# A third block product done in seven smaller ones, over two feature tiles

## The chip, the cores and the metric

The kernel runs on one core of a Trainium2 chip. The metric is the device time of one execution in microseconds, as the median of several runs. Its engines are TensorE (PE in the profile, with PEld for its weight loads), VectorE (DVE), ScalarE (ACT), GpSimd (POOL) and SyncE (SP), which here issues the DMAs. Every engine works through its own instructions in order and waits on semaphores for the others.

## What is computed

One inference step of a hybrid decoder layer on 1048 tokens (16 learned ones, 1024 of a prompt, 8 samples) of width 1024. The layer has a half-step feed-forward block, a mixing block (HGRN2 and Mamba-2 heads) and a second half-step feed-forward block. The change lies in the two feed-forward blocks (FFN), which are

```python
def rmsnorm(x, w):
    xf = x.astype(jnp.float32)
    y = xf * lax.rsqrt(jnp.mean(xf * xf, axis=-1, keepdims=True) + EPS)
    return (y * w.astype(jnp.float32)).astype(x.dtype)

def swiglu(x, wg, wu, wd):
    return (jax.nn.silu(x @ wg) * (x @ wu)) @ wd
...
    h = h + 0.5 * swiglu(rmsnorm(h, n1), w1g, w1u, w1d)
...
    h = h + 0.5 * swiglu(rmsnorm(h, n2), w2g, w2u, w2d)
```

with `wg` and `wu` (1024, 2816) and `wd` (2816, 1024), all in float32. So there are 22 feature tiles of 128 columns in `wg` and `wu`.

## The kernel before

**Numbers.** Each float32 operand is split into a high part (a cast to the format that TensorE takes, on ScalarE) and a low part (the difference, on VectorE). A product is three matmuls, high by high, high by low and low by high: `mm3`, lines 163 to 165.

**Gate and up in block form.** For one feature tile, gate and up together are a 2 by 2 block product: the left side is gate and up by the two halves of the 1024 input features (four raw weight blocks of 128 by 512), the right side the input by the same halves and by two parts of the tokens. `Left`, `Unit` and `pair` do this with Strassen's seven block products instead of eight (in Winograd's arrangement): `ORDER = (1, 6, 2, 5, 7, 3, 4)`, line 334. The right operands and their sums are made once (`Blocks`) and stay, 28 slots of the ring "u" with 30 slots; one more holds the scaling of the norm (`Spread`). Left operands 1, 7, 4 and 2 are the raw blocks, 5, 6, 7 and 3 are sums of them (`Left.sum_`, L482). Each block product is done for two token halves c = 0 and 1, a step each: 4 row tiles × 3 matmuls = 12 matmuls of 262 columns (258 in the second FFN). A feature tile has 14 steps.

**The order.** `Steps` is a list of steps. `S.before(i, fn)` puts work ahead of step i, `post` comes right behind a step's matmuls, and jobs of one step come in the order in which they were registered. VectorE, ScalarE, TensorE and SyncE keep this order (`manual_schedule` in `ffn`). For a tile that begins at step s0, `Left.plan` puts the loads at s0−11 and s0−10, the sums at s0−7 to s0−5, the cast of the k-th product (`hi`, L486) at s0+2k−4 and its low part (`lo`, L490) one step later.

**Evacuation.** Product sums lie in PSUM, in two pairs of banks (`psum2`) while gate and up run; products 2, 3 and 4 add to the banks of 1, 5 and 7 after these have been read. `post` in `pair`: product 1 is copied (ScalarE, L574), 6, 5, 7, 3 and 4 are added to what is there (VectorE, L576, L583, L585, L587, L593), gate and up are scaled by `spread` (L569), silu runs on ScalarE (L581, L602), and the products go to the hidden slots (L608). `Hidden` forms four sums of the hidden blocks of two tiles (L734) and stores seven blocks (L737), from which the down product's operands are loaded later (`Hidden.load`, with low parts of 1048 columns at L762).

**Rings.** Raw weights "r" 8 slots, temporaries "t" 9, split weights "ws" 6, "s" 8 (hidden blocks and their sums). Four more PSUM banks (`psm`) aren't used by steady gate and up.

**Loops.** `ffn` runs over 11 pairs of feature tiles. In the first FFN, pair 0 is done without Strassen's form (`Plain`) and pairs 1 to 10 by `pair`; in the second all 11 go through `pair`, the first tile in another order (`first`). Then `down` follows; its first operand loads and low parts are put into the last steps of gate and up (14 to 2 steps ahead).

Of the kernel before, what the change touches and what calls it, by code (L numbers as in the profile page):

```python
# [9 lines left out]
F32 = mybir.dt.float32  # L10
F32R = mybir.dt.float32r
# [6 lines left out]
P = 128  # L18
# [421 lines left out]
class Steps:  # L440
# [9 lines left out]
    def add(self, mm, post=None):  # L450
        self.steps.append((mm, post))

    def run(self):
        for i, (mm, post) in enumerate(self.steps):
            for fn in self.at.pop(i, ()):
                fn()
            mm()
            if post:
                post()
        for i in sorted(self.at):  # L460
            for fn in self.at[i]:
                fn()


class Left:

    def __init__(self, K, srcs, n):
        self.K, self.n = K, n  # L470
        self.srcs = dict(zip((1, 7, 4, 2), srcs))
        self.raw, self.w = {}, {}

# [4 lines left out]
    def sum_(self, p):  # L478
        x, y, op = {5: (7, 4, ALU.add), 6: (5, 1, ALU.subtract), 7: (1, 7, ALU.subtract), 3: (2, 6, ALU.subtract)}[p]
        if p not in self.raw:  # L480
            self.raw[p] = self.K.raw(self.n * P)
        self.K.nc.vector.tensor_tensor(self.raw[p], self.raw[x], self.raw[y], op)  # L482

    def hi(self, p):
# [8 lines left out]
        self.hi(p)  # L493
        self.lo(p)

    def plan(self, S, s0, late, sums):
        for ps, ds, fn in (
            ((1, 7, 4, 2), (-11, -11, -10, -10), self.load),
            ((5, 6, 7, 3), [d + sums for d in (-7, -7, -6, -5)], self.sum_),
            (ORDER, [2 * i - 4 + late for i in range(7)], self.hi),  # L500
            (ORDER, [2 * i - 3 + late for i in range(7)], self.lo),
        ):
            for p, d in zip(ps, ds):
                S.before(s0 + d, lambda p=p, fn=fn: fn(p))
# [9 lines left out]
class Unit:  # L514


    def __init__(self, K, w, ops, n, post):
        self.K, self.w, self.ops, self.n, self.post = K, w, ops, n, post
        self.ps = {}

    def bank(self, p, cs, mis):
# [10 lines left out]
    def step(self, S, p, c, cs, mis=False):  # L532
        def mm():
            new = p in (1, 6, 5, 7)
            b = self.bank(p, cs, mis)
            product(self.K, b[:, cs.index(c)], self.w[p], self.ops[c][p], self.n, new, True, not new)

        S.add(mm, (lambda: self.post(p, slice(cs[0], cs[-1] + 1), self.bank(p, cs, mis))) if c == cs[-1] else None)

    def both(self, S):  # L540
        for p in ORDER:
# [158 lines left out]
            S.before(at + i, lambda fn=fn, n=n: fn(n))  # L700


FP = DFF // P // 2

DORDER = (1, 5, 6, 7, 3, 4, 2)
# [3 lines left out]
class Hidden:  # L709
# [6 lines left out]
    def jobs(self, S, i, hid, e0, e1):  # L716

        K = self.K
        t, b = {}, {}

        def block(n):

            return hid[n // 2][0][:, n % 2 * 2 * self.K.Q : n % 2 * 2 * self.K.Q + 2 * self.K.Q]

        def val(p):
            return b[p] if p in b else block({1: 0, 12: 1, 2: 2, 3: 3}[p])

        def sub(p, x, y):
# [5 lines left out]
            K.nc.vector.tensor_sub(b[p], val(x), val(y))  # L734

        def store(p):
            K.nc.sync.dma_start(self.d[p][:, :, i, :], halves(val(p)))  # L737

        ks = (1, 3, 5) if i < FP - 1 else (1, 2, 3)
        for at, args in zip((e0 + 1, *(e1 + k for k in ks)), ((5, 12, 1), (6, 3, 5), (7, 3, 12), (4, 2, 6))):  # L740
            S.before(at, lambda args=args: sub(*args))
            S.before(at + 2, lambda p=args[0]: store(p))
        for at, p in ((e0 + 2, 1), (e1 + 1, 3), (e1 + 2, 2)):
            S.before(at, lambda p=p: store(p))

    def load(self, S, p, at):

# [147 lines left out]
def ffn(K, wg, wu, wd, ops, spread, src, first, after, late_r, plain=False):  # L895
# [1385 lines left out]
```

## Time and profile before

| | us |
|---|---|
| median of 3 runs (1946.39 to 1948.55) | 1947.09 |
| span of the profiled execution | 1943.5 |
| TensorE busy in the span | 1921.7 |
| TensorE weight loads busy | 1887.7 |
| VectorE busy | 1434.7 |
| ScalarE busy | 823.6 |
| GpSimd busy | 90.3 |

The profile is of one execution; the page gives its span, from the first to the last instruction, and no time of its own. Busy TensorE is modelled from the starts of matmuls, so 99% says that it always has work, not that it is at its peak. The granted clock is 0.997 over the span. In a row of the order of time stand the start, the length, the engine, the line, the operation, what it writes and reads, and in brackets how long the engine had been idle and who released it. "x2" merges two neighbours, with the length of both.

### The profile page before, as it was taken

To read this page: it belongs to the slowest core of one execution; us is meant where nothing else is said; L and a number is where in the kernel's file an instruction comes from. 1 tells how busy PE (TensorE), PEld (TensorE's weight loads), DVE (VectorE), ACT (ScalarE), POOL (GpSimd) and SP (SyncE) were. 2 spreads that over 40 slices of the span, in tenths; PEclk is the share of its full clock that TensorE was granted. 3 is DMA by queue.
4 is the path that set the end of the run, shared out by engine and by line. 5 is a ranking of instruction groups with operands and counts; after the bars stand their busy time and mean duration, and the time that the engine had idled before them with its cause. 6 is when DMAs were issued, how large, how long until landed. Compare 5 with 4: busy or idle time off the path is not lost.

```text
span 1943.5 us, 41139 instructions
## 1 busy us (share of the span) xinstructions
PE 1921.7 (99%) x16800; PEld 1887.7 (97%) x16800; DVE 1434.7 (74%) x2516; ACT 823.6 (42%) x1558; POOL 90.3 (5%) x144
## 2 busy tenths in 40 slices
PE   9999999999999999999999999999999999999998
PEld 8999999999999999999899999999999999999998
DVE  7877777778688877576575556987777777768974
ACT  7522222224543644466564545742222222354343
POOL 3000000000000510000000002200000000000000
PEclk9999999999999999999999999999999999999999
DMA  8142332325977541221453254223332433487852
GB/s 246 47 129 83 101 114 83 114 85 157 289 230 257 172 146 53 64 88 48 117 160 93 79 176 137 91 80 99 94 104 82 124 90 100 153 257 231 280 182 86
DMA packets 324207, 258.45 MB, mean 133 GB/s; under 512 B 18923, under 2 KB 298731, under 8 KB 324011
## 3 DMA queue, kind: packets, MB, share of 16 engines
q1 hardware_dynamic: 323779, 255.79, 43.4%
q8 instruction: 132, 2.16, 0.4%
q14 instruction: 56, 0.46, 0.1%
q0 software_dynamic: 224, 0.04, 0.0%
q10 hardware_dynamic: 16, 0.00, 0.0%
HBM read 190.79 MB, written 65.05 MB: 132 GB/s over the span
## 4 chain that ended last, share of the span: by engine, by line
PE 93%; DVE 4%; issue 1%; ACT 1%; DMA 1%; SPq 0%; POOL 0%; DVEq 0%; ACTq 0%; POOLq 0%
PE acc L163 29%; PE acc L164 28%; PE acc L165 28%; PE mis L1677 1%; PE mis L1390 0%; DVE u L376 0%; PE mis L1739 0%; PE mis L1384 0%; DMA s<-in_x_prompt_dram 0%; DVE ws L490 0%; DVE t L321 0%; PE mis L1768 0%; PE mis L1377 0%; PE mis L1668 0%; PE mis L223 0%
## 5 line engine op out<-in xcount | busy, mean ns | idle before, releaser
L163 PE MATMUL acc<-u,ws 128*128 128x258 f32 (+3 forms) x4514 | 1316.4, 292 | 5.6 <-DVE t L583 2.3
L165 PE MATMUL acc<-u,ws 128*128 128x258 f32 (+3 forms) x4514 | 1304.0, 289 | 1.3 <-DVE ws L490 1.3
L164 PE MATMUL acc<-u,ws 128*128 128x258 f32 (+3 forms) x4514 | 1304.8, 289 | 0.2 <-DVE u L324 0.2
L163 PEld LDWEIGHTS acc<-u,ws 128*128 128x128 f32 x4514 | 852.6, 189 | 15.3 <-issue 10.0
L164 PEld LDWEIGHTS acc<-u,ws 128*128 128x128 f32 x4514 | 854.9, 189 | 1.4 <-DVE u L324 0.7
L165 PEld LDWEIGHTS acc<-u,ws 128*128 128x128 f32 x4514 | 852.2, 189 | 2.6 <-DVE ws L490 2.1
L490 DVE TENSOR_TENSOR ws<-r,ws 128x512 fp32r<-128x512 f32 x302 | 208.4, 691 | 69.6 <-ACT ws L486 69.5
L486 ACT CAST ws<-r 128x512 fp32r<-128x512 f32 x302 | 170.3, 614 | 4.8 <-DVE r L482 4.8
L602 ACT ACTIVATE t<-t 128x516 f32<-128x516 f32 (+1 forms) x43 | 27.4, 640 | 289.3 <-DVE t L569 289.3
L482 DVE TENSOR_TENSOR r<-r,r 128x512 f32<-128x512 f32 x168 | 115.7, 690 | 8.4 <-DMA r<-in_w_ffn_up_dram 6.8
L581 ACT ACTIVATE t<-t 128x516 f32<-128x516 f32 (+1 forms) x41 | 26.2, 639 | 197.2 <-DVE t L569 197.2
L762 DVE TENSOR_TENSOR u<-u,u 128x1048 fp32r<-128x1048 f32 (+3 forms) x84 | 97.2, 1158 | 9.8 <-ACT u L758 9.8
L250 POOL TENSOR_TENSOR t<-t,t 128x262 f32<-128x262 f32 (+1 forms) x56 | 58.2, 1048 | 783.2 <-DMA u<-hd 601.3
L158 DVE TENSOR_TENSOR ws<-r,ws 128x512 fp32r<-128x512 f32 x88 | 60.9, 700 | 40.6 <-ACT ws L157 40.1
L569 DVE TENSOR_TENSOR t<-t,u 128x516 f32<-128x516 f32 (+1 forms) x127 | 85.1, 697 | 2.8
L758 ACT CAST u<-u 128x1048 fp32r<-128x1048 f32 (+3 forms) x84 | 83.0, 988 | 4.0 <-DMA u<-hd 4.0
L820 ACT CAST ws<-u 128x512 fp32r<-128x512 f32 (+1 forms) x72 | 42.1, 585 | 98.9 <-DVE u L815 96.8
L825 DVE TENSOR_TENSOR ws<-r,ws 128x512 fp32r<-128x512 f32 (+1 forms) x84 | 56.3, 679 | 29.4 <-ACT ws L820 29.4
L849 DVE SCALAR_TENSOR_TENSOR s<-acc,s 128x524 f32<-128x524 f32 (+3 forms) x86 | 53.8, 649 | 32.8 <-PE acc L165 32.5
L820 ACT CAST ws<-r 128x512 fp32r<-128x512 f32 (+1 forms) x84 | 48.0, 582 | 65.1 <-DVE r L815 30.2
L574 ACT COPY t<-acc 128x516 f32<-128x516 f32 (+2 forms) x43 | 25.0, 582 | 103.5 <-PE acc L165 102.5
L569 DVE TENSOR_TENSOR t<-acc,u 128x516 f32<-128x516 f32 (+1 forms) x41 | 28.7, 699 | 49.5 <-PE acc L165 49.5
(420 smaller groups left out, 1844.8 us busy)
## 6 DMA issues: line engine op xcount, KB each, us to landing
r<-in_w_ffn_down_dram SPq DMA_DIRECT2D x128, 256.0 KB
hd<-s SPq DMA_DIRECT2D x93, 258.0 KB
r<-in_w_ffn_gate_dram SPq DMA_DIRECT2D x88, 256.0 KB
r<-in_w_ffn_up_dram SPq DMA_DIRECT2D x88, 256.0 KB
hd<-s SPq DMA_DIRECT2D x77, 262.0 KB
u<-hd SPq DMA_DIRECT2D x36, 516.0 KB
u<-hd SPq DMA_DIRECT2D x28, 524.0 KB
r<-in_w_in_dram SPq DMA_DIRECT2D x56, 256.0 KB
```

What stands on the lines that cost most here:

```text
L158: self.nc.vector.tensor_sub(lo, src, hi.bitcast(F32))
L163: mm(ps, whi, xhi, start=first, stop=False, skip_group_check=more)
L164: mm(ps, whi, xlo, start=False, stop=False, skip_group_check=more)
L165: mm(ps, wlo, xhi, start=False, stop=last, skip_group_check=more)
L250: K.nc.gpsimd.tensor_add(self.sq[q], self.sq[q], t)
L482: self.K.nc.vector.tensor_tensor(self.raw[p], self.raw[x], self.raw[y], op)
L486: self.K.nc.scalar.copy(self.w[p][:, : self.n * P], self.raw[p])
L490: self.K.nc.vector.tensor_sub(t[:, 512 : 512 + w], self.raw[p], t[:, :w].bitcast(F32))
L569: nc.vector.tensor_mul(t, t if src is None else src, spread.lanes(i, cs))
L758: K.nc.scalar.copy(hi, lo.bitcast(F32))
L762: K.nc.vector.tensor_sub(lo, lo.bitcast(F32), hi.bitcast(F32))
L820: nc.scalar.copy(w[p, j, g][:, : n * P], src)
```

## The change

Pair 1 of the first FFN and pair 0 of the second stay with `pair`. All later pairs (9 in the first FFN, 10 in the second) go through the new `two_pairs`:

- A tile has six products instead of seven, `ORDER2 = (1, 6, 2, 5, 7, 4)`, so 12 steps for 14. Product 7 is read after each token half, since product 4 now adds to its banks right behind it.
- Product 3 of both tiles is one more 2 by 2 block product: left, the two tiles by two halves of 512 rows; right, the two token halves. It is done once more in Strassen's form (`Third`), seven small products of 2 × 3 matmuls in the order `SUB = (1, 6, 2, 7, 5, 3, 4)`, behind the steps 3 to 9 of the second tile. They use the four `psm` banks. Their result (`q`) takes a slot "s" and is added to both tiles' second gate block in `second`.
- The right sums of these small products are made once, in nine steps from late_r+14 (`SubBlocks`), from the split operand 3, and keep three slots of "s" and one of "u".
- The first tile's raw sum for product 3 takes a slot of ring "t" instead of "r" until `Third` has split it. The left sums of the small products are of half width.
- Loads of a tile are at −11, −10, −10 and −9, in the order 7, 4, 1, 2 (before: −11, −11, −10, −10, in the order 1, 7, 4, 2). The seven stores of a pair go out over the steps 4 to 9 behind the pair (`jobs_apart`), one at step 2 of the second tile.

The core of the diff:

```diff
     def sum_(self, p):
...
-            self.raw[p] = self.K.raw(self.n * P)
+            self.raw[p] = (self.K.t if p in self.apart else self.K.raw)(self.n * P)
...
+ORDER2 = (1, 6, 2, 5, 7, 4)
+SUB = (1, 6, 2, 7, 5, 3, 4)
+class SubBlocks:
...
+        todo = [
+            [(join, 5, 0, 0)],
+            [(join, 7, 0, 1), (sub, 5, 7, 5)],
+            [(cast, 5), (join, 6, 1, 1)],
+            [(low, 5), (sub, 7, 6, 7)],
+            [(sub, 6, 6, 5), (cast, 7)],
+            [(low, 7), (cast, 6)],
+            [(low, 6), (join, 4, 1, 0)],
+            [(sub, 4, 4, 6), (cast, 4)],
+            [(low, 4)],
+        ]
...
+class Third:
+    def plan(self, S, s1):
+        for d, fn, *args in (
+            (-2, self.sums, 0),
+            (-1, self.sums, 1),
+            (0, self.hi, 0),
+            (1, self.lo, 0),
+            (1, self.hi, 1),
+            (2, self.lo, 1),
+            (2, self.sums, 2),
+            (3, self.hi, 2),
+            (4, self.lo, 2),
+            (5, self.hi, 3),
+            (6, self.lo, 3),
+        ):
+            S.before(s1 + d, lambda fn=fn, args=args: fn(*args))
...
+    def mm(self, m):
...
+        x = self.sub.right(m)
+        for k in range(2):
+            ks = slice(k * K.Q, k * K.Q + K.Q)
+            wh, wl = (self.w[t][:, d + o + k * P : d + o + k * P + P] for d in (0, 512))
+            K.mm3(self.ps[b], wh, wl, x[0][:, ks], x[1][:, ks], m == b and k == 0, k == 1, m != b)
+
+    def post(self, m):
...
+        if m == 1:
+            self.v = halves(K.t(2 * K.Q))
+            nc.scalar.copy(self.v[:, 0], ps[1])
+        elif m == 6:
+            nc.vector.tensor_add(self.v[:, 0], ps[6], self.v[:, 0])
+        elif m == 2:
+            q = K.slot("s", 4 * K.Q)
+            self.q = [halves(q[:, f * 2 * K.Q : f * 2 * K.Q + 2 * K.Q]) for f in range(2)]
+            nc.scalar.copy(self.q[0][:, 0], ps[1])
+        elif m == 5:
+            nc.vector.tensor_add(self.v[:, 1], ps[5], self.v[:, 0])
+            nc.vector.tensor_add(self.q[1][:, 1], ps[7], self.v[:, 1])
+        elif m == 3:
+            nc.vector.tensor_add(self.q[0][:, 1], ps[5], self.v[:, 0])
+        elif m == 4:
+            nc.vector.tensor_add(self.q[1][:, 0], ps[7], self.v[:, 0])
...
+def two_pairs(K, S, wg, wu, i, ops, spread, hids, sub):
...
+    def gate(f, n, t, src):
+        nc.vector.tensor_mul(t, src, spread.lanes(n, cs))
+        nc.scalar.activation(t, t, AF.Silu)
+
+    def out(f, n, u):
+        nc.vector.tensor_mul(u, u, spread.lanes(n, cs))
...
+        nc.vector.tensor_mul(halves(hids[f][0][:, n * 2 * K.Q : n * 2 * K.Q + 2 * K.Q]), temp(f, f"g{n}"), u)
...
+        elif p == 4:
+            u = temp(f, "v")
+            nc.vector.tensor_add(u, b, u)
+            out(f, 0, u)
+
+    def second(f):
+        g = temp(f, "g1")
+        nc.vector.tensor_add(g, g, third.q[f])
+        gate(f, 1, g, g)
...
+    for f in range(2):
+        unit = Unit(K, lefts[f].w, [o.op for o in ops], 4, lambda p, c, b, f=f: post(f, p, c, b), (7,))
+        for p in ORDER2:
+            for c in range(2):
+                j = len(S.steps) - s1
+                unit.step(S, p, c, (0, 1))
+                if 3 <= j < 10:
+                    S.also(lambda m=SUB[j - 3]: third_step(m))
+    S.before(s1 + 10, lambda: second(0))
+    S.before(s1 + 11, lambda: out(0, 1, temp(0, "u1")))
+    S.before(s1 + 12, lambda: second(1))
+    S.before(s1 + 13, lambda: out(1, 1, temp(1, "u1")))
...
+    def jobs_apart(self, S, i, hid, s1):
+
+        n = s1 + 12
+        last = i == FP - 1
+        sums = (0, 2, 3, 4) if last else (0, 2, 4, 6)
+        stores = (2, 3, 4, 4, 5, 6) if last else (4, 5, 6, 7, 8, 9)
+        sub, store = self.parts(i, hid)
+        for d, args in zip(sums, ((5, 12, 1), (6, 3, 5), (7, 3, 12), (4, 2, 6))):
+            S.before(n + d, lambda args=args: sub(*args))
+        S.before(s1 + 2, lambda: store(1))
+        for d, p in zip(stores, (5, 3, 6, 2, 7, 4)):
+            S.before(n + d, lambda p=p: store(p))
...
+        sub = SubBlocks(K, ops)
+        sub.jobs(S, late_r + 14)
         for i in range(int(plain), NF // 2):
             hid, e = [], []
+            if i > int(plain):
+                hid = [[], []]
+                hidden.jobs_apart(S, i, hid, two_pairs(K, S, wgv, wuv, i, ops, spread, hid, sub))
+                continue
```

Here s1 is the first step of the second tile of a pair, so s1+12 is the first step of what follows.

More of the change, by code (lines that the diff above doesn't have):

```diff
@@ L451, in add, with also @@
         self.steps.append((mm, post))
+    def also(self, fn):
+        mm, post = self.steps[-1]
+        self.steps[-1] = (mm, lambda: (post and post(), fn()))
     def run(self):
@@ L465, with __init__ @@
 class Left:
-    def __init__(self, K, srcs, n):
-        self.K, self.n = K, n
+    def __init__(self, K, srcs, n, apart=()):
+        self.K, self.n, self.apart = K, n, apart
         self.srcs = dict(zip((1, 7, 4, 2), srcs))
@@ L494, in split, with plan @@
         self.lo(p)
-    def plan(self, S, s0, late, sums):
+    def plan(self, S, s0, late, sums, order=ORDER, loads=(-11, -11, -10, -10)):
         for ps, ds, fn in (
-            ((1, 7, 4, 2), (-11, -11, -10, -10), self.load),
+            ((7, 4, 1, 2) if len(order) == 6 else (1, 7, 4, 2), loads, self.load),
             ((5, 6, 7, 3), [d + sums for d in (-7, -7, -6, -5)], self.sum_),
-            (ORDER, [2 * i - 4 + late for i in range(7)], self.hi),
-            (ORDER, [2 * i - 3 + late for i in range(7)], self.lo),
+            (order, [2 * i - 4 + late for i in range(7)], self.hi),
+            (order, [2 * i - 3 + late for i in range(7)], self.lo),
         ):
@@ L514, with __init__ @@
 class Unit:
-    def __init__(self, K, w, ops, n, post):
-        self.K, self.w, self.ops, self.n, self.post = K, w, ops, n, post
+    def __init__(self, K, w, ops, n, post, apart=()):
+        self.K, self.w, self.ops, self.n, self.post, self.apart = K, w, ops, n, post, apart
         self.ps = {}
@@ L536, in mm @@
             product(self.K, b[:, cs.index(c)], self.w[p], self.ops[c][p], self.n, new, True, not new)
-        S.add(mm, (lambda: self.post(p, slice(cs[0], cs[-1] + 1), self.bank(p, cs, mis))) if c == cs[-1] else None)
+        if p in self.apart:
+            S.add(mm, lambda: self.post(p, slice(c, c + 1), self.bank(p, cs, mis)[:, c : c + 1]))
+        else:
+            S.add(mm, (lambda: self.post(p, slice(cs[0], cs[-1] + 1), self.bank(p, cs, mis))) if c == cs[-1] else None)
     def both(self, S):
@@ L737, in store, with jobs @@
             K.nc.sync.dma_start(self.d[p][:, :, i, :], halves(val(p)))
+        return sub, store
+    def jobs(self, S, i, hid, e0, e1):
+        sub, store = self.parts(i, hid)
         ks = (1, 3, 5) if i < FP - 1 else (1, 2, 3)
```

103 lines of the change are left out of this document (102 added, 1 removed).

## The prediction

> **What bounds the kernel now.** I read the page's busy table and its chain of waits first, then busy time by stage, then the order of time on VectorE and ScalarE inside one pair of feature tiles.
>
> ```profile
> span 1943.5 us, 41139 instructions
> PE 1921.7 (99%) x16800; PEld 1887.7 (97%) x16800; DVE 1434.7 (74%) x2516; ACT 823.6 (42%) x1558; POOL 90.3 (5%) x144
> PE acc L163 29%; PE acc L164 28%; PE acc L165 28%; PE mis L1677 1%; PE mis L1390 0%; DVE u L376 0%; PE mis L1739 0%; PE mis L1384 0%; DMA s<-in_x_prompt_dram 0%; DVE ws L490 0%; DVE t L321 0%; PE mis L1768 0%; PE mis L1377 0%; PE mis L1668 0%; PE mis L223 0%
> ```
>
> TensorE is the bound: 85% of the chain is the three matmul lines of `mm3`. A matmul taken out of it is worth its spacing, as long as its operands stay on time. The two gate-and-up stretches (columns: length, then busy time of PE, PEld, DVE, ACT):
>
> ```profile
> 92.00:483.80 391.80, 390.25 (x3208) 390.06 (x3207) 300.75 (x464) 111.37 (x201) 0.00 (x0) 1.00 0.37 109
> 1285.00:1708.00 423.00, 423.00 (x3531) 422.89 (x3530) 326.90 (x507) 123.12 (x222) 0.20 (x1) 1.00 0.36 105
> 258.90 0.60 ACT L574 COPY t<-acc 128x524 f32<-128x524 f32 x1 [2.70 <-PE acc L165]
> 279.33 0.60 ACT L574 COPY t<-acc 128x524 f32<-128x524 f32 x1 [2.70 <-PE acc L165]
> ```
>
> The copy at L574 comes once in a feature tile, after product 1: 279.33 − 258.90 = 20.43 us for 14 steps of 12 matmuls, so 121.6 ns a matmul and 1.459 us a step in the first FFN (262 columns); in the second 423.00/3531 = 119.8 ns (258 columns). In these stretches VectorE is the second engine, 77% busy (300.75/391.80), and it works in the order written in the code. How it paces itself:
>
> ```profile
> 274.22 1.32 DVE L569 TENSOR_TENSOR t<-t,u 128x524 f32<-128x524 f32 x2
> 276.14 0.69 DVE L490 TENSOR_TENSOR ws<-r,ws 128x512 fp32r<-128x512 f32 x1 [0.60 <-ACT ws L486]
> 276.75 0.70 DVE L593 TENSOR_TENSOR t<-acc,t 128x524 f32<-128x524 f32 x1
> 277.48 0.70 DVE L569 TENSOR_TENSOR t<-t,u 128x524 f32<-128x524 f32 x1
> 278.22 1.32 DVE L608 TENSOR_TENSOR s<-t,t 128x524 f32<-128x524 f32 x2
> 279.58 0.70 DVE L734 TENSOR_TENSOR s<-s,s 128x524 f32<-128x524 f32 x1
> 280.20 0.68 DVE L490 TENSOR_TENSOR ws<-r,ws 128x512 fp32r<-128x512 f32 x1
> 280.80 0.70 DVE L734 TENSOR_TENSOR s<-s,s 128x524 f32<-128x524 f32 x1
> 65.92 0.42 DVE L678 COPY s<-acc 128x262 f32<-128x262 f32 x1
> 66.26 0.68 DVE L482 TENSOR_TENSOR r<-r,r 128x512 f32<-128x512 f32 x1
> 274.96 0.64 ACT L602 ACTIVATE t<-t 128x524 f32<-128x524 f32 x1 [7.30 <-DVE t L569]
> 275.51 1.12 ACT L486 CAST ws<-r 128x512 fp32r<-128x512 f32 x2
> ```
>
> An operation over 512 or 524 columns starts 0.61 us after the one ahead (276.14 to 276.75, 280.20 to 280.80); if it reads that one's result, 0.73 to 0.74 (276.75, 277.48, 278.22). Half a width takes 0.34 (65.92 to 66.26). A silu starts 0.74 after the multiply before it (274.22 to 274.96), a cast 0.55 after the silu, the low part (L490) 0.63 after its cast (275.51 to 276.14). What a late VectorE does to TensorE is in the chain at the start of these pairs:
>
> ```profile
> 104.64 0.70 DVE r L482
> 105.97 0.71 DVE t L583
> 106.68 0.14 issue
> 106.82 0.36 PE acc L163
> L165 PE MATMUL acc<-u,ws 128*128 128x262 f32 x1809 | 513.4, 284 | 1.1 <-DVE ws L490 1.1
> ```
>
> A late sum (104.64) made the evacuation of product 5 late (105.97), and TensorE went on 0.14 us after its end: a bank not yet read stops it, and so does a low part not yet written (last row).
>
> **The change part by part.** *Matmuls.* Per pair of tiles product 3 cost 2 tiles × 2 halves × 12 = 48; in its place come 7 products of 6 = 42. 9 pairs in the first FFN and 10 in the second are changed: 54 × 0.1216 + 60 × 0.1198 = 13.8 us less. A pair has 330 matmuls, 40.13 us for 40.86.
>
> *VectorE's work.* In full widths and halves a pair had 14 low parts, 8 sums, 22 evacuations, scalings and products, 4 sums of `Hidden`: 48 full. Now it has 15 low parts, 8 sums, 20 evacuations and scalings, 4 of `Hidden` = 47 full, and 14 halves (4 left sums, 1 low part, 4 for product 7, 5 for the seven small products). That is 47 × 0.61 + 14 × 0.34 = 33.4 us for 29.3, plus what dependence adds: about 85% of 40.13 us. Over the pair it fits; where it stands does not.
>
> *The seam between two pairs.* In the second tile seven steps carry a small product each and last 2.19 us; the steps from its last two into the next tile have none, and there `second` and `out` of both tiles, `post` of product 4 and the next tile's low parts stand in a row. Take 0 where TensorE begins the step s1+10, just after the last small product, whose evacuation VectorE can start at 0.26 (a matmul ends 0.28 after its start, the last starts 0.12 before 0, and 0.1 to notice, a little under the 0.14 at 106.68). Then, by the spacings above: 0.26 evacuation (half), 0.60 `second` add, 1.34 multiply, 1.95 scaling of u1, 2.75 product (it waits for the silu: 1.34 + 0.74 + 0.64 + 0.04), 3.37 low part of product 6, 3.98 product 4's add (TensorE had finished it at 2.92), 4.71 scaling, 5.45 product, 6.06 `second` add of the other tile, 6.80 multiply, 7.41 sum of `Hidden`, 8.03 scaling, 8.77 product, 9.38 low part of product 2, ready at 10.07. VectorE has no pause in it. TensorE needs that low part for the third matmul of the sixth step from 0: 6 × 1.459 + 2 × 0.1216 = 9.00. With 0.14 to go on, it comes 1.2 us late. ScalarE is late too: its silu starts at 7.54, the cast at 8.09, the copy of product 1 at 8.62, 0.60 long (row at 258.90); product 2 may use that bank at 9.36 instead of 8.75. That 0.6 lies within the 1.2. Queued behind the low part on VectorE are the next sums and low parts; they are needed two steps apart and catch up by 17 us. There are 8 seams in the first FFN and 9 in the second, where the steps are shorter (six of them 8.63, so 1.3): 8 × 1.2 + 9 × 1.3 = 21.3 us. Bounds: 0.6 a seam if only the bank waits, 10.2; 2.0 if every operation cost the dependent spacing (0.735 for 13 of them, the row's end at 10.95 and 11.0 against 9.0), 34.
>
> *Rule and row.* By the Trainium skill, VectorE: DVE Perf Modes, section "The DRAIN you can't avoid", an operation does not start until the one before has left the pipe. That speaks against a change with 13 operations more in a pair; read strictly, every spacing would be the whole 0.70 or more, and this term would be its upper bound. The rows have starts 0.61 apart with records 0.69 long, so I go by the rows.
>
> *Operands of the small products.* `SubBlocks` puts 12 operations of 524 columns into nine steps: 12 × 0.615 = 7.4 us against 9 × 1.459 × 23% = 3.0 us that VectorE is idle there. 4.4 us too much, of which the slack of the next steps takes some: 3 us in the first FFN (0 to 4.4); in the second it falls on the first changed pair, together with three sums of `Hidden`: 4.5 (0 to 7.4).
>
> *Into the down product.* There six low parts of up to 1.26 us stand in the last second tile, beside the small products:
>
> ```profile
> L762 DVE TENSOR_TENSOR u<-u,u 128x1048 fp32r<-128x1048 f32 x28 | 35.4, 1263 | 5.7 <-ACT u L758 5.7
> L476 SPq DMA_DIRECT2D r<-in_w_ffn_gate_dram x88: 367/458/1053, 2.7 to 1671.4; - x88
> L737 SPq DMA_DIRECT2D hd<-s x154: 512/529/1741, 76.2 to 1714.6; - x154
> ```
>
> I take 1.2 us each, one small product's wait for its bank, 2.4 together (0 to 5).
>
> *At nothing.* Loads and stores are as many as before, 8 and 7 a pair at about 0.5 us of SyncE's queue (rows above), 8 of 40 us. The loads now go out ahead of the stores, three or four steps (4.4 to 5.8 us) before their first sum. A store waits for VectorE's sums, 1 to 2 us later than now, and behind the stores wait no loads for five steps. Were that cover gone, a load would hold a sum as at 104.64, 1.8 us once. The raw sums of product 3 in the other ring, the 16 casts a pair for 14 (ScalarE is 28% busy), and the four small banks, unused here so far, cost nothing; ScalarE's one wait for a weight slot, at the step s1+5, ends two steps before its use.
>
> *Sum.* −13.8 + 21.3 + 3 + 4.5 + 2.4 = +17.4 us. The profiled execution's span is 1943.5, and the median of the runs is 1947.09, so 3.6 us lie around it: 1943.5 + 17.4 = 1960.9, as a time 1964.5.
>
> **Rivals.** *The whole gain arrives:* no step waits longer than now, 1947.1 − 13.8 = 1933.3. For it: over a pair VectorE keeps a fifth of its time free, and ScalarE two thirds. Against it: the row of 14 operations up to the low part, 9.1 us from 0.26, and the 9.00 by which it is needed. It decides at 0.73 us: if a seam costs less than the six matmuls of a pair, and the start and end little, the kernel is faster.
>
> *Only the bank waits:* low parts are in time, and 17 × 0.6 = 10.2 stays, with 3 us at the starts: 1947.1 − 13.8 + 13.2 = 1946.5, no change. For it: 0.6 us less on VectorE ahead of that low part is enough. Against it: in that row of work no operation is free to go.
>
> *Every operation at the dependent spacing* (what the skill's rule would make of it): 34 in place of 21.3, 1977.2. Against it: the rows.
>
> *A wait for a slot of a ring:* three of the eight slots "s" stay taken until the end of gate and up, five are left and five are used a pair. If the next pair's first tile had to wait for the last store, up to 1 us a seam more: 1982. For it: a store is issued up to 9 steps behind the pair. Against it: its slot is asked for again two steps or more later.
>
> **How the numbers follow.** The forecast, VectorE late at the seam, has 0.68; the whole gain 0.12; the bank alone 0.10; the dependent spacing 0.04; the slots 0.06. The time is the forecast's, 1964.5, its own range 1953 to 1974 (1.0 to 1.5 us a seam, and the two starts between 3 and 9). For 8 in 10 the range goes to 1938 below, into the cases with part of a wait, and to 1978 above, the dependent spacing; left out are the whole gain and the slots. A measurement of this kernel can tell 0.2%, 3.9 us, from no change. Faster by more: 0.15 (the whole gain, and a little of the bank case); within: 0.08; slower: 0.77.
>
> **What would show it.** In the changed profile a pair would be 41.2 to 41.5 us from one copy of product 1 to that of the next pair, with 330 matmuls; TensorE would stand at the third and fourth matmul of product 2 of each first tile, released by ScalarE's copy and by VectorE's low part; VectorE would have no idle time from the last small evacuation to that low part. Wrong I would be if the pair is 40.1 us long, if VectorE's row has gaps, or if the waits are at a DMA or a slot instead.

## The result, and the profile after

The changed kernel takes 2020.94 us (median of 5 runs, 2018.56 to 2023.18) against 1948.51 us for the kernel before in the same session (1946.39 to 1948.98): a ratio of 1.0376, interval 1.0364 to 1.0389. It is 72.4 us slower; 17.4 were forecast.

The page of the changed kernel: span, busy time, shares of the chain of waits by engine, and three groups of instructions (the idle time just before them and what ended it stand last). In the changed kernel the low parts are L495, the half reads of product 7 L904.

```profile
span 2019.8 us, 41324 instructions
PE 1937.9 (96%) x16686; PEld 1886.4 (93%) x16686; DVE 1537.6 (76%) x2787; ACT 859.2 (43%) x1642; POOL 84.7 (4%) x144
...
PE 74%; DVE 20%; issue 3%; ACT 2%; DMA 1%; POOL 0%; SPq 0%; DVEq 0%; ACTq 0%; POOLq 0%
...
L163 PE MATMUL acc<-u,ws 128*128 128x258 f32 (+4 forms) x4210 | 1241.4, 295 | 54.4 <-DVE t L904 40.7
L165 PE MATMUL acc<-u,ws 128*128 128x258 f32 (+4 forms) x4210 | 1223.4, 291 | 9.7 <-DVE ws L495 9.7
...
L904 DVE TENSOR_TENSOR t<-acc,t 128x258 f32<-128x258 f32 (+1 forms) x76 | 32.6, 428 | 43.8 <-PE acc L165 41.9
```

There are 114 matmuls fewer (16686 for 16800), and yet a fifth of the chain now lies on VectorE, where it was 4% before. TensorE waits 9.7 us for low parts, which were forecast, and 40.7 us for L904, which stands nowhere in the sum. L904 in its turn waits 41.9 us for TensorE: the two take turns.

Busy time in one pair, from one copy of product 1 to that of the next pair's first tile, in the first and the second FFN (columns: length, then PE, PEld, DVE, ACT), before:

```profile
177.16:218.03 40.87, 40.87 (x338) 40.87 (x337) 30.99 (x49) 11.01 (x20) 0.00 (x0) 1.00 0.34 98
1405.36:1445.63 40.27, 40.27 (x338) 40.27 (x337) 30.75 (x49) 10.97 (x21) 0.00 (x0) 1.00 0.34 99
```

and after:

```profile
171.30:215.25 43.95, 41.39 (x333) 40.51 (x332) 35.57 (x62) 12.61 (x26) 0.00 (x0) 1.00 0.30 92
1436.46:1479.95 43.49, 40.91 (x333) 40.05 (x332) 35.33 (x62) 12.53 (x26) 0.00 (x0) 1.00 0.30 92
```

(Matmuls that reach over an edge are counted too.) A pair lost its six matmuls and got 3.1 to 3.2 us longer, at a granted clock of 1.00 before and after. VectorE has 4.6 us more work, and the pair still has room for it: 35.57 of 43.95 us.

The order of time on VectorE at a seam of the changed kernel (start, length):

```profile
162.95 0.43 DVE L857 TENSOR_TENSOR s<-mis,t 128x262 f32<-128x262 f32 x1 [0.30 <-PE mis L165]
163.30 0.69 DVE L912 TENSOR_TENSOR t<-t,s 128x524 f32<-128x524 f32 x1
...
166.07 0.68 DVE L495 TENSOR_TENSOR ws<-r,ws 128x512 fp32r<-128x512 f32 x1
166.68 0.70 DVE L907 TENSOR_TENSOR t<-acc,t 128x524 f32<-128x524 f32 x1
...
171.54 0.70 DVE L892 TENSOR_TENSOR s<-t,t 128x524 f32<-128x524 f32 x1
172.16 0.68 DVE L495 TENSOR_TENSOR ws<-r,ws 128x512 fp32r<-128x512 f32 x1
```

and TensorE there, in the order of time of the same kernel:

```profile
171.51 0.28 PE L165 MATMUL acc<-u,ws 128*128 128x262 f32 x1
171.94 0.39 PE L163 MATMUL acc<-u,ws 128*128 128x262 f32 x1 [0.15 <-ACT t L896]
172.16 0.28 PE L164 MATMUL acc<-u,ws 128*128 128x262 f32 x1
172.90 0.39 PE L165 MATMUL acc<-u,ws 128*128 128x262 f32 x1 [0.46 <-DVE ws L495]
```

This is the forecast seam: a row without a pause, 9.21 us from the small evacuation to the low part (forecast 9.12), then the copy of product 1 (L896) holds the first matmul of product 2 and the low part its third. Two starts lie 0.43 and 0.74 us behind the ones before them where 0.12 is usual: 0.93 us lost, and about 0.2 more because the start right behind each of the two comes 0.10 us late (0.22 apart).

The wait that wasn't forecast stands 8 us later, in the same tile. TensorE, still in the order of time:

```profile
179.94 0.28 PE L165 MATMUL acc<-u,ws 128*128 128x262 f32 x1
181.56 0.39 PE L163 MATMUL acc<-u,ws 128*128 128x262 f32 x1 [1.33 <-DVE t L904]
...
183.00 0.28 PE L165 MATMUL acc<-u,ws 128*128 128x262 f32 x1
183.90 0.36 PE L163 MATMUL acc<-u,ws 128*128 128x262 f32 x1 [0.61 <-DVE t L904]
```

and VectorE at that time:

```profile
179.05 0.69 DVE L495 TENSOR_TENSOR ws<-r,ws 128x512 fp32r<-128x512 f32 x1
179.66 0.68 DVE L487 TENSOR_TENSOR r<-r,r 128x512 f32<-128x512 f32 x1
180.26 0.70 DVE L902 TENSOR_TENSOR t<-acc,t 128x524 f32<-128x524 f32 x1
181.07 0.43 DVE L904 TENSOR_TENSOR t<-acc,t 128x262 f32<-128x262 f32 x1
181.41 0.68 DVE L495 TENSOR_TENSOR ws<-r,ws 128x512 fp32r<-128x512 f32 x1
183.32 0.43 DVE L904 TENSOR_TENSOR t<-acc,t 128x262 f32<-128x262 f32 x1 [1.22 <-PE acc L165]
```

From 171.94 to 179.94 TensorE starts 60 matmuls, five steps of 12: both halves of products 2 and 5, and the first half of product 7. So the matmul at 181.56 is the first of product 7's *second* half. It waits until VectorE has read the *first* half (181.07, 0.43 long), though the halves lie in different banks. At 183.32 it is VectorE that stands, for the second half, and then product 4 (183.90) for that read. Starts 1.62 and 0.90 us apart: 2.28 us lost in a pair. In the second tile a small product of six matmuls stands between the halves and covers the read.

### The profile page after: what moved, and what is told of

It reads as the page before. It is cut to its first block, busy times and chain, and to the rows that moved or that the text cites. A ratio compares the mean times of both kernels' runs of the same rounds, so it can differ in the third digit from the quotient of the medians.

```text
span 2019.8 us, 41324 instructions
## 1 busy us (share of the span) xinstructions
PE 1937.9 (96%) x16686; PEld 1886.4 (93%) x16686; DVE 1537.6 (76%) x2787; ACT 859.2 (43%) x1642; POOL 84.7 (4%) x144
## 4 chain that ended last, share of the span: by engine, by line
PE 74%; DVE 20%; issue 3%; ACT 2%; DMA 1%; POOL 0%; SPq 0%; DVEq 0%; ACTq 0%; POOLq 0%
PE acc L163 21%; PE acc L165 20%; PE acc L164 20%; DVE r L487 3%; DVE ws L495 2%; DVE s L965 2%; DVE s L892 2%; DVE t L885 2%; PE mis L163 2%; PE mis L165 2%; PE mis L164 2%; DVE t L889 1%; DVE t L912 1%; DVE t L904 1%; DVE t L902 1%
## 5 line engine op out<-in xcount | busy, mean ns | idle before, releaser
L163 PE MATMUL acc<-u,ws 128*128 128x258 f32 (+4 forms) x4210 | 1241.4, 295 | 54.4 <-DVE t L904 40.7
L165 PE MATMUL acc<-u,ws 128*128 128x258 f32 (+4 forms) x4210 | 1223.4, 291 | 9.7 <-DVE ws L495 9.7
L164 PE MATMUL acc<-u,ws 128*128 128x258 f32 (+4 forms) x4210 | 1221.2, 290 | 1.1 <-DVE u L376 0.8
L163 PEld LDWEIGHTS acc<-u,ws 128*128 128x128 f32 x4210 | 797.0, 189 | 77.2 <-DVE t L904 32.2
L165 PEld LDWEIGHTS acc<-u,ws 128*128 128x128 f32 x4210 | 797.3, 189 | 15.2 <-DVE ws L495 14.7
L164 PEld LDWEIGHTS acc<-u,ws 128*128 128x128 f32 x4210 | 799.7, 190 | 2.4 <-DVE u L376 1.1
L495 DVE TENSOR_TENSOR ws<-r,ws 128x512 fp32r<-128x512 f32 x264 | 182.4, 692 | 15.7 <-ACT ws L491 15.5
L886 ACT ACTIVATE t<-t 128x516 f32<-128x516 f32 (+1 forms) x76 | 48.6, 640 | 338.0 <-DVE t L885 338.0
L491 ACT CAST ws<-r 128x512 fp32r<-128x512 f32 x264 | 152.9, 616 | 4.8 <-DVE r L487 4.7
L487 DVE TENSOR_TENSOR r<-r,r 128x512 f32<-128x512 f32 x149 | 102.9, 692 | 5.1 <-DMA r<-in_w_ffn_up_dram 3.7
L158 DVE TENSOR_TENSOR ws<-r,ws 128x512 fp32r<-128x512 f32 x88 | 60.9, 701 | 38.7 <-ACT ws L157 38.3
L820 ACT CAST ws<-t 128x512 fp32r<-128x512 f32 (+1 forms) x57 | 31.2, 547 | 133.3 <-DVE t L809 85.6
L1098 DVE SCALAR_TENSOR_TENSOR s<-acc,s 128x524 f32<-128x524 f32 (+3 forms) x86 | 53.9, 650 | 31.7 <-PE acc L165 31.4
L163 PE MATMUL mis<-u,ws 128*128 128x258 f32 (+1 forms) x228 | 65.0, 285 | 2.2 <-DVE t L852 2.0
L904 DVE TENSOR_TENSOR t<-acc,t 128x258 f32<-128x258 f32 (+1 forms) x76 | 32.6, 428 | 43.8 <-PE acc L165 41.9
L1074 DVE TENSOR_TENSOR ws<-u,ws 128x512 fp32r<-128x512 f32 (+1 forms) x72 | 47.4, 659 | 23.7 <-ACT ws L1069 23.7
```

The lines of the kernel that those rows point to most:

```text
L158: self.nc.vector.tensor_sub(lo, src, hi.bitcast(F32))
L163: mm(ps, whi, xhi, start=first, stop=False, skip_group_check=more)
L164: mm(ps, whi, xlo, start=False, stop=False, skip_group_check=more)
L165: mm(ps, wlo, xhi, start=False, stop=last, skip_group_check=more)
L491: self.K.nc.scalar.copy(self.w[p][:, : self.n * P], self.raw[p])
L495: self.K.nc.vector.tensor_sub(t[:, 512 : 512 + w], self.raw[p], t[:, :w].bitcast(F32))
```

## The experiments

Each ratio is against the kernel before, run in the same session on the same chip. `after` below is the changed kernel, ratio 1.0376.

**Product 7 in tiles of its own.** In the first tile of a pair each token half of products 7 and 4 gets one of the four small banks as a tile of its own, instead of a half of a two-bank tile. VectorE reads the same things in the same order; only product 4's evacuation becomes two halves. The core of the edit:

```diff
...
+        if self.own and b == 7:
+            if b not in self.ps:
+                self.ps[b] = [self.K.psm()[:, None, : self.K.Q] for _ in range(2)]
+            return self.ps[b]
...
```

> In the first tile of a changed pair, products 7 and 4 get a PSUM tile of their own for each token half (two of the four small banks), in place of one tile of two banks. Theory A (the read of one half of product 7 holds TensorE back from the other half, because both lie in one PSUM tile): the second half of product 7 follows the first without a pause, both waits of the first tile (1.49 and 0.78 us plus restarts) go; what stays is the seam, 0.93 us plus restarts. A pair takes 41.5 us instead of 43.94, and 19 pairs make 2021 - 19 x 2.4 = 1975 us. Rival B (VectorE is simply late at product 7, whichever bank it reads): product 4 waits for the same late reads, a step later; a pair stays above 43 us and the time above 2010.

Measured 1978.44 us, ratio 1.0162 (1.0132 to 1.0191): 0.0214 less than `after`, 41.7 us. TensorE's largest waits, in the view of waits (waited in all, times, longest):

```profile
PE acc L165 <- DVE ws L495: 9.6, 23, 0.5
PE mis L163 <- DVE t L912: 5.5, 2, 3.5
```

The waits at product 7's reads are gone and the seam's are as before: of 40.7 us on that read nothing is left but the second row, product 4 waiting in the first changed tile of each stretch, where VectorE is late for other reasons (below). In the middle of a changed stretch VectorE reads the first half

```profile
216.46 0.43 DVE L912 TENSOR_TENSOR t<-mis,t 128x262 f32<-128x262 f32 x1
```

while matmuls of the second half start at 216.57, 216.70 and 216.81. So in the changed kernel the second half was held by the read of the first because both are one tile to the program's dependencies, not because the chip needs it. (By the Trainium skill, PSUM — Partial Sum Buffer, section "Summary: rules for kernel authors", a bank should be read while matmuls run in a different bank, and guarded bank by bank; this run agrees, 41.7 us between guarding by the two-bank tile and by the bank.)

**Product 7 read once.** The other way to be rid of the wait between its halves: one read behind both, so that only product 4 can wait.

```diff
-        unit = Unit(K, lefts[f].w, [o.op for o in ops], 4, lambda p, c, b, f=f: post(f, p, c, b), (7,))
+        unit = Unit(K, lefts[f].w, [o.op for o in ops], 4, lambda p, c, b, f=f: post(f, p, c, b))
```

> Product 7 is read once, both halves together, as in the kernel before; everything else as changed. Theory A: no wait between the halves; one wait ahead of product 4 in each tile, from the end of the last matmul over 0.12 to notice, 0.70 for the full read and 0.14 to go on: 1.1 us in the first tile, 0.4 in the second, where a small product lies between. A pair takes about 43.0 us, the time is about 2004. Rival B: the read comes later than the first half's does now, so the wait ahead of product 4 grows: 2021 or more.

Measured 1993.02 us, ratio 1.0237 (1.0207 to 1.0267). TensorE's waits:

```profile
PE acc L163 <- DVE t L904: 23.4, 38, 2.9
PE acc L165 <- DVE ws L495: 9.4, 22, 0.5
```

One wait of 1.04 us in the first tile and one of 0.32 in the second take the place of 2.28: 1.36 a pair, 40.7 us down to 23.4. The time is about 10 us better than expected. One part of that is at the seam, where the wait for the bank nearly vanished (0.1 us for 0.31 in the pair at 209 us) and the one for the low part stays; that the second tile has one evacuation less ahead of it would explain it, but no run shows it alone.

**The seam.** The second tile's `second` and `out` two steps later, so that the next tile's low parts go first, with the hidden sums and stores behind them (not for the last pair).

```diff
-    S.before(s1 + 12, lambda: second(1))
-    S.before(s1 + 13, lambda: out(1, 1, temp(1, "u1")))
+    d = 0 if i == FP - 1 else 2
+    S.before(s1 + 12 + d, lambda: second(1))
+    S.before(s1 + 13 + d, lambda: out(1, 1, temp(1, "u1")))
...
-        sums = (0, 2, 3, 4) if last else (0, 2, 4, 6)
-        stores = (2, 3, 4, 4, 5, 6) if last else (4, 5, 6, 7, 8, 9)
+        sums = (0, 2, 3, 4) if last else (6, 8, 9, 10)
+        stores = (2, 3, 4, 4, 5, 6) if last else (8, 9, 10, 11, 12, 13)
```

> The changed kernel with second and out of the second tile two steps later, the four hidden sums at steps 6, 8, 9, 10 behind the pair (before 0, 2, 4, 6) and the stores at 8 to 13, except behind the last pair. The theory of the prediction (fourteen VectorE operations in a row make the copy of product 1 and the low part of product 2 late): these two waits go, 17 x 1.1 us, and the waits at product 7 stay: about 2000 us. Rival (VectorE is short over the whole pair, a wait that is taken away comes back further on): within 6 us of 2021.

Measured 2001.55 us, ratio 1.0281 (1.0251 to 1.0311): 0.0095 less than `after`, 18.5 us.

```profile
PE acc L163 <- DVE t L904: 35.2, 38, 3.4
PE mis L163 <- DVE t L852: 6.1, 2, 3.3
```

The seam is worth nearly what was forecast for it. The 18.5 us are net: the second row, a small product's wait for its bank in the last pair of each FFN, has grown from 2.0 us in `after` to 6.1. The waits at product 7 hardly fell, 40.7 to 35.2 us. So they are not the seam's backlog, passed on; they are a cost of their own.

**The half reads in the kernel before.** The kernel before, with product 7 read after each half, nothing else.

```diff
-        S.add(mm, (lambda: self.post(p, slice(cs[0], cs[-1] + 1), self.bank(p, cs, mis))) if c == cs[-1] else None)
+        if p == 7 and len(cs) == 2:
+            S.add(mm, lambda: self.post(p, slice(c, c + 1), self.bank(p, cs, mis)[:, c : c + 1]))
+        else:
+            S.add(mm, (lambda: self.post(p, slice(cs[0], cs[-1] + 1), self.bank(p, cs, mis))) if c == cs[-1] else None)
```

> The kernel before with one thing of the change alone: product 7 is read after each half. Theory A: in each of 41 tiles (20 in the first FFN, 21 in the second) the second half waits for the read of the first, 0.28 + 0.12 + 0.43 + 0.14 - 0.12 = 0.85 us: 1948.5 + 35 = 1983. Rival B: VectorE has time at that place in the kernel before, and the halves are in different banks: within 3 us of 1948.5.

Measured 2030.26 us, ratio 1.0428 (1.0384 to 1.0472), far above both numbers. The page's group of the matmul that waits, and one such place on VectorE (L586 is product 5's evacuation, L588 product 7's):

```profile
L163 PE MATMUL acc<-u,ws 128*128 128x258 f32 (+3 forms) x4514 | 1325.0, 294 | 67.0 <-DVE t L588 64.7
```

```profile
223.81 1.42 DVE L482 TENSOR_TENSOR r<-r,r 128x512 f32<-128x512 f32 x2 [0.25 <-DMA r<-in_w_ffn_up_dram]
225.14 0.70 DVE L586 TENSOR_TENSOR t<-acc,t 128x524 f32<-128x524 f32 x1
225.75 0.68 DVE L482 TENSOR_TENSOR r<-r,r 128x512 f32<-128x512 f32 x1
226.35 0.42 DVE L588 TENSOR_TENSOR t<-acc,t 128x262 f32<-128x262 f32 x1
```

TensorE stood 1.53 us for the read at 226.35 and went on at 226.83. Without any seam, in a kernel that leaves VectorE a quarter of its time idle over a pair, a tile still loses about 1.5 us (a copy of product 1 every 21.9 us for 20.43): ahead of the read stand sums and product 5's evacuation, put into the same steps, and there is no slack left for them (the first of these sums also came 0.25 us late for its load). What was too small in the expectation was the lateness of VectorE, not the mechanism; the rival, that a half read costs nothing here, falls. Six tiles lost 3.5 to 4.6 us: in each TensorE stood 2.2 to 3.4 us, and around the end of that wait its granted clock fell to half for 3.4 us, once for 6.8 (the last section has the rows).

**Both repairs at once.** Tiles of their own, and the seam.

> Both repairs at once: product 7 and 4 of the first tile in banks of their own, and the second tile's second gate block and the hidden sums later. Theory A (two separate waits a pair, one at product 7, one at the seam, which add up): neither stays, a pair is about 40.4 us in the first FFN and 40.1 in the second (40.86 and 40.27 before). 9 x -0.5 and 10 x -0.2 us are -6.5; with the starts of the two stretches, which were longer by 5.8 and 7.6 us in the run with the seam alone repaired, and 3 at their ends, +9.9: about 1957 us. Rival B (VectorE has too much work in a pair, and the waits come back at another place): a pair of 41.7 or more, 1975 us or more.

Measured 1960.98 us, ratio 1.0066 (1.005 to 1.0082). Busy time in a pair of each FFN:

```profile
204.08:244.45 40.37, 40.37 (x332) 40.30 (x331) 35.34 (x63) 12.72 (x24) 0.00 (x0) 1.00 0.33 99
1437.79:1477.68 39.89, 39.89 (x332) 39.82 (x331) 35.02 (x63) 12.64 (x25) 0.00 (x0) 1.00 0.34 100
```

They add up: 1.0376 − 0.0214 − 0.0095 = 1.0067. TensorE is busy through the pair, which is 0.50 and 0.38 us *shorter* than before, with VectorE at 88% (35.34/40.37). What is left of the loss is at the starts and ends of the two stretches; the total is 4 us above the expected 1957.

**The operands of the small products over more steps.** As the run before, `SubBlocks` in every second step.

```diff
-                S.before(at + i, lambda fn=fn, args=args: fn(*args))
+                S.before(at + 2 * i, lambda fn=fn, args=args: fn(*args))
```

> As the run with both repairs, and the operands of the small products (SubBlocks) made over 17 steps, every second step, in place of nine. Theory C (the longer starts are VectorE, which has 7.4 us of work in nine steps where it is idle for 3.0): over 17 steps it is idle for 5.7, so that about 2 us are left of each start; 10 us less than with both repairs, about 1947. Rival D (the starts are longer because of the first changed pair's own loads, sums and small products): no change against both repairs, about 1957.

Measured 1957.87 us, ratio 1.0048 (1.0033 to 1.0063): 3 us less, not 10. VectorE got its room, but did not use it:

```profile
122.12 0.68 DVE L495 TENSOR_TENSOR ws<-r,ws 128x512 fp32r<-128x512 f32 x1
125.10 1.43 DVE L487 TENSOR_TENSOR r<-r,r 128x512 f32<-128x512 f32 x2 [2.29 <-DMA r<-in_w_ffn_up_dram]
```

It stood 2.29 us for a load of weights in the first FFN and 2.07 in the second, for a sum of the pair's second tile, and the evacuations of the first stand behind it: TensorE then waited 2.77 and 4.42 us at product 4 of the first changed tile. Neither theory had this.

**`SubBlocks` alone.** The kernel before, with the operands of the small products made in the same nine steps but not used.

> The kernel before, with the operands of the small products made in the same nine steps but not used. As predicted blind, these cost 3 + 4.5 us: 1954.5 us. Theory C: the whole of what the starts were longer by, 13 us: about 1960. Rival D: within 2 us of the kernel before, 1948.

Measured 1956.39 us, ratio 1.004 (1.0026 to 1.0054), 8.4 us. Copies of product 1 on ScalarE around the first start, in this kernel

```profile
94.83 0.60 ACT L574 COPY t<-acc 128x524 f32<-128x524 f32 x1 [1.62 <-PE acc L165]
141.78 0.60 ACT L574 COPY t<-acc 128x524 f32<-128x524 f32 x1 [2.70 <-PE acc L165]
```

and in the kernel before:

```profile
93.62 0.60 ACT L574 COPY t<-acc 128x524 f32<-128x524 f32 x1 [1.62 <-PE acc L165]
136.30 0.60 ACT L574 COPY t<-acc 128x524 f32<-128x524 f32 x1 [2.70 <-PE acc L165]
```

Two tiles take 46.95 us for 42.68: 4.3 in the first FFN, 3.7 in the second by the same reading. The forecast 3 + 4.5 was right in sum; theory C, that these operands are the whole of the longer starts, falls.

**The stores at the start.** The wait for a load has its reason in SyncE's queue, here of the changed kernel:

```profile
123.64 0.51 SPq L968 DMA_DIRECT2D hd<-s  x1
124.24 0.56 SPq L481 DMA_DIRECT2D r<-in_w_ffn_up_dram  x1
124.86 0.56 SPq L968 DMA_DIRECT2D hd<-s  x1
125.51 0.56 SPq L481 DMA_DIRECT2D r<-in_w_ffn_up_dram  x1
```

The pair ahead of the first changed one is still a `pair`, and its stores (L968), each behind a hidden sum of a late VectorE, stand in turn with the loads (L481) of the first changed pair's second tile. So its stores were moved behind these loads, first in the changed kernel and then in the one with the operands spread:

```diff
-            S.before(at + 2, lambda p=args[0]: store(p))
-        for at, p in ((e0 + 2, 1), (e1 + 1, 3), (e1 + 2, 2)):
+        for at, p in ((e0 + 2, 1), (e0 + 3, 5), (e1 + 4, 3), (e1 + 5, 6), (e1 + 6, 2), (e1 + 7, 7), (e1 + 8, 4)):
             S.before(at, lambda p=p: store(p))
```

The edit moves the stores of pair 0 of the first FFN too, which goes through the same lines.

> The changed kernel, with the stores of the one pair ahead of the first changed one moved behind the loads of that pair's second tile (steps 4 to 8 instead of 1 to 7), nothing else. Theory E (at the two starts the loads stand in SyncE's queue behind a store that waits for a late sum on VectorE; a sum of weights then waits for its load, 3.7 us in the first FFN): that wait is gone or under 1 us, TensorE stands 2 to 4 us less at each start, together about 5 us less than the changed kernel: 2016. Rival F (the load is late for its own length, or the sum is late for VectorE's work alone): no change, 2021.

> As the run with both repairs and the operands of the small products over 17 steps, with the same stores moved. Theory E: the waits of VectorE for a load (2.3 and 2.1 us) go, and with them TensorE's waits of 3.1 and 4.7 us at the first changed pair's small products; about 7 us less, 1951. Rival G (VectorE is behind there in any case, since the operands of the small products stand in the same steps): less than 2 us, 1956 or more.

The first measured 2016.34 us, ratio 1.0361 (1.0344 to 1.0378): 0.0015 less than `after`, 2.9 us, with intervals that overlap. In its queue the two loads of `up` (at 124.24 and 125.51 above) go out without a store between them and 13 to 16 us earlier, of which 3.4 us already lie ahead of this place:

```profile
107.86 4.93 SPq L481 DMA_DIRECT2D r<-in_w_ffn_up_dram  x2
```

Inside the profiles the first FFN's start is 3.7 us shorter (the first changed pair and what it waits for take 44.3 us for 48.0), and VectorE's wait of 3.7 us for a load is gone there; the second FFN had no such wait in the changed kernel, and won nothing. The second measured 1951.12 us, ratio 1.0023 (1.0014 to 1.0033), by the ratios 0.0025 or 4.9 us less than without it, nearer to theory E's 7 than to rival G (the times are 6.8 us apart, but in two sessions): both loads are in time, as theory E had it (TensorE's wait was at product 4 of the first tile, not at a small product as the expectation says; 2.2 us of it stay in the second FFN). So part of the late start came from the order in SyncE's queue, where work of VectorE that is late holds a load, through a store.

**The ends.** What remains are waits of the last pair's small products, 3.0 and 2.8 us from start to start where 0.12 is usual, beside the low parts for the down product.

```diff
-        sums = (0, 2, 3, 4) if last else (6, 8, 9, 10)
-        stores = (2, 3, 4, 4, 5, 6) if last else (8, 9, 10, 11, 12, 13)
+        sums = (0, 2, 3, 4) if last else (1, 4, 5, 6) if i == FP - 2 else (6, 8, 9, 10)
+        stores = (2, 3, 4, 4, 5, 6) if last else (4, 6, 7, 8, 9, 10) if i == FP - 2 else (8, 9, 10, 11, 12, 13)
```

> As the run before it, with the hidden sums of the pair ahead of the last one at the steps 1, 4, 5 and 6 in place of 6, 8, 9 and 10, ahead of the low parts for the down product. Theory H (the wait of 3.4 us at a small product of the last pair, once in each FFN, comes from the hidden sums pushed into the same steps as those low parts): about 2 us less at each end, 1947, which would be the time of the kernel before. Rival I (ScalarE waits there for a slot of the split weights, and the low parts behind it are late whatever VectorE does before): no change against the run before it.

Measured 1948.5 us, ratio 1.0007 (0.9997 to 1.0016), 2.6 us less: two thirds of the expected 4. The last pair's starts are now about 1.3 us apart, and another such gap of 1.3 us came up at product 4 in the tile before, so theory H holds for a part.

**Only the pairs in between.** The first and the last of the changed pairs stay with `pair`; `SubBlocks` begins 14 steps later and takes every third step. The later stores stay for the one pair ahead of the first changed one.

```diff
...
-        sub.jobs(S, late_r + 14)
+        sub.jobs(S, late_r + 28)
...
-            if i > int(plain):
+            if int(plain) + 1 < i < FP - 1:
...
```

> As the run before it, but only the pairs 3 to 9 of the first FFN and 2 to 9 of the second in the changed form: one pair more ahead of them stays as it was, with the operands of the small products made over 25 steps there (every third), and the last pair too, so that no small products stand beside the low parts for the down product. Theory J (what is left above the kernel before is start and end alone, about 1.6 + 2.4 us of TensorE's waits at the two starts and 3.3 at each end, while a pair in between gives 0.5 or 0.4 us): 7 x 0.5 + 8 x 0.37 = 6.5 us less than the kernel before, of which 2 to 3 go at the starts: about 1943, a ratio of 0.998. Rival K (VectorE, at its limit in the changed pairs, gives the gain back at whichever pairs are the first and the last): no change against the run before it, 1947 to 1949.

Measured 1940.36 us (6 runs, 1938.03 to 1941.87), ratio 0.9967 (0.9955 to 0.9979): faster than both kernels. TensorE's waits for VectorE in the feed-forward blocks are now nearly those of the kernel before (2.3 us there for product 5's evacuation, 1.3 for low parts):

```profile
PE acc L163 <- DVE t L599: 2.3, 2, 1.6
...
PE acc L165 <- DVE ws L495: 1.4, 4, 0.5
```

Of the 7.3 us by which its span (1936.2) is shorter than 1943.5, the two changed stretches give 3.7 and 1.1; 2.6 lie between them, in the mixing block, where the program is the same. In the profile before, 3.4 us of that block ran at half the granted clock (0.50 from 756 to 759 us), in this one none of it; an estimate from the matmuls' spacing, 0.22 us for 0.12 at half clock, is 1.5 us of the 2.6 if TensorE sets the pace there, and the rest stays open. So 4.8 us is what the small products are shown to be worth.

## Why the prediction was right in sign and wrong in size

**The matmuls** (−13.8): right in count. Without waits a pair is 0.50 and 0.38 us shorter, where 0.73 was forecast. A pair of 40.37 us is 0.24 above 330 × 0.1216; where it goes among the small products was not followed further, and over 19 pairs, with 0.36 in the second FFN, it makes 6 us.

**The seam** (+21.3): right, in mechanism, place and size. The row's starts, taken from 162.69, agree with the working within 0.1 us to its end, the dependent operations 0.73 or 0.74 apart and the others 0.61 or 0.62, which also settles the rival of the dependent spacing. TensorE lost 0.93, with what follows the waits 1.1, for the 1.2 forecast, and undoing the seam gave back 18.5 us.

**What is late next** is the step that failed: "Queued behind the low part on VectorE are the next sums and low parts; they are needed two steps apart and catch up by 17 us." Two things were wrong in it. What stands there is not only sums and low parts but also the evacuation of products 5 and 7; and it is needed at 17 us sharp, not two steps later: TensorE came to the end of product 7's first half 17.3 us after the seam's zero (179.94 against 162.69), and VectorE then still had product 5's evacuation ahead (180.26), and read at 181.07. The prediction named the half reads in its count of VectorE's work ("4 for product 7") and asked only what they cost VectorE. It never asked which matmul waits for each of them. That is the larger part of the miss: even with an idle VectorE the second half would wait 0.85 us, by the estimate in the expectation of the half reads in the kernel before, where 1.50 us were lost; the late queue adds the rest. By the two-bank tile it is product 7's own second half, then product 4: 2.28 us a pair, 41.7 us in all. That alone is three quarters of the missing 55 us. The sign was not luck: without this wait the kernel is still 31.7 us slower than the one before (1978.44 us).

**`SubBlocks`** (+7.5): right, 8.4 alone in the kernel before.

**Loads and stores** (at nothing): wrong at one place. "The loads now go out ahead of the stores" is true between changed pairs; at the first one the pair ahead is an old one, with stores at its old steps. There the cover that the prediction named was gone, and the price that it set, 1.8 us once, became 3.7 us in the first FFN.

**Into the down product** (+2.4): near. The waits measure 1.17 and 0.53 us at each end (starts 1288 and 654 ns apart for 120), 3.4 us in all, and the second kind, a bank of the down product, had not been named.

**The sum.** −13.8, and then 6 for the longer pair without waits, 18.5, 41.7, 8.4, 3.7 and 3.4, make 68 of the 72.4 us. The rest is not settled; 3.1 us of the profiled difference lie ahead of the changed region, at the first loads, where 3.4 us also ran at half the granted clock (0.50 from 17.5 to 20.5 us).

**The rivals.** None happened as told, and the time lies beyond all of them. The signs announced were a pair of 41.2 to 41.5 us and stalls at product 2 alone; the profile has 43.95, and the stalls at product 2 and at product 7. "The whole gain arrives" was the wrong forecast and the right goal: at 0.73 us a seam it was said to decide, and the last kernel has less than that at each.

## What to carry to other kernels

When a read of PSUM is split or moved, ask for each new read which matmul waits for it, and what the dependency covers: a tile of two banks makes the second bank's matmuls wait for the first bank's read. An engine's free time over a loop says that its work fits in; a deadline at every step says whether it is in time, so follow its queue until it has been idle once, and past the point where you would like to stop. A gain of six matmuls a pair is kept only if the first and the last of the changed rounds, which meet loads, stores and set-up work of their neighbours, are looked at on their own.

## What the runs showed of the hardware that was not expected

TensorE often does not go on at its full pace after a wait: the second matmul starts 0.22 us after the first (171.94 and 172.16, 181.56 and 181.78), where 0.12 is usual. It is so behind three of the four waits of that pair, 0.3 us on top of the waits themselves; behind the fourth (183.90) it is not.

After a long wait the granted clock can fall to half. In the run with half reads in the kernel before, a stretch ahead of one such wait (TensorE stands until 181.18) and one behind it (columns as above; the granted clock is third from the end):

```profile
160.00:177.00 17.00, 17.00 (x142) 17.00 (x141) 12.02 (x19) 4.99 (x10) 0.00 (x0) 1.00 0.35 100
183.00:186.00 3.00, 3.00 (x16) 3.00 (x15) 1.03 (x2) 0.00 (x0) 0.00 (x0) 0.50 0.00 0
```

There the matmuls start 0.22 us apart for 0.12. In these traces such a stretch lasts 3.4 us, or 6.8, and costs by that spacing about 1.5 us for each 3.4. The wait of 4.42 us in the run with the operands spread is followed by one, and so are the waits of about 3 us at the ends of the run with both repairs; the last kernel, whose longest wait in the changed stretches is 1.6 us, has none. It is not a rule: a wait of 2.9 us in the run with one read has none behind it, and the kernel before has one in its mixing block without a long wait ahead. In the profiled executions the changed kernel ran 6.8 us at half clock and the run with the seam 17.1, counted up to the last matmul, so the 18.5 us of the seam are rather too few.
